# A hybrid attention layer: x given transposed beside x, weights laid out chunk by chunk, squares of x moved behind the first product

## The chip, the cores and the metric

The kernel runs on one core of a Trainium2 chip. The metric is device time in microseconds (us) of one execution; lower is better. The engines named below: TensorE (PE, with its weight loads as PEld), VectorE (DVE), ScalarE (ACT), GpSimd (POOL), and SyncE (SP), whose queue issues most transfers.

## What is computed

One decoder layer on x of 256 rows by 1024 columns, float32: an RMS norm, one wide projection, causal softmax attention with 8 heads of 64 (with 256 rows there is one key block, so the block choice selects nothing), gated linear attention with 4 heads, a merge by sigmoid gates, an output projection, the residual and a final RMS norm. Cut to what matters here:

```python
h = rms_norm(x, norm_in_g[layer])              # x * rsqrt(mean(x*x) + eps) * g
proj = jnp.einsum('bsd,de->bse', h, w_in[layer])
(mq, mk, mv, mgate, gq, gk, gv, ggate, gfg, ga, gb) = jnp.split(proj, split_pts, axis=-1)
...
oa = oa.transpose(0, 2, 1, 3).reshape(B, S, MOBA_WIDTH) * jax.nn.silu(mgate)
...
merged = (jax.nn.sigmoid(ga + b_merge[layer, 0]) * ya
          + jax.nn.sigmoid(gb + b_merge[layer, 1]) * yb)
x = x + jnp.einsum('bsd,de->bse', merged, w_out[layer])
return rms_norm(x, norm_f_g)
```

## The kernel before

**Products in three parts.** Each float32 product is made of three matmuls in the type float32r: both operands are split into a rounded part and a rest, `hi` and `lo` for weights, `xh` and `xl` for x, and hi·xh, hi·xl and lo·xh are added up in PSUM (`three`, L709). A weight chunk is loaded into a ring of five buffers (`raw`, L152), then cast on ACT to `hi` (L174) and subtracted on DVE to `lo` (L175), into rings of five each. `load_to(n)` and `split_to(n)` issue loads and splits up to chunk n - 1; `prefetch(i)` calls both some chunks ahead. All loads of chunks go through SP's queue.

**Chunks and groups.** `group` (L115) cuts the weights. Group mg (kind K) has 8 chunks, 0 to 7, of 128 rows by 512 columns, one for each k (a slice of 128 of the 1024 columns of x); they lie in a buffer of their own, `first`. Group gg (kind G) has chunks 8 to 11, two k each, 528 columns; gqk has chunks 12 to 15; then come mq, mk, mv, gv, ga, gb, the two projections and the output. TensorE runs the groups in this order.

**The start.** x is loaded in five pieces between the chunks of mg (L193), five matmuls on zeros follow (`warm`, L235), the norm's weights come as 8 rows and are turned into columns of `vecs` by a transpose (L270). `x_part(k)` (L246) transposes the slice k of x by two TensorE transposes into PSUM, multiplies it with the norm's weight into `xh` on ACT, and makes `xl` on DVE. In the mg loop (L716) every k runs 12 matmuls, and after two of its four column blocks `x_part(k + 2)` and `split_to` are issued. `squares` (L260, ACT) is issued at k = 5 and k = 6.

**The norm's factor.** It is not multiplied into x, but into the results. `gates_mg` (L332) is started after the mg loop: `rms` makes rs = (mean + eps)^-0.5, the power on POOL (L268); two `diag` tiles; a transpose of `b_merge`; four short matmuls `ones` x `diag` that spread rs over all partitions (L343); a copy to `rB` on ACT (L345); four multiplications `mgz` of mg's results with rB (L348); sigmoid and so on.

**The order.** The order on every engine is that of the program, which plans it with a clock of its own: a matmul of n columns adds n/2400, a side function's `yield t` lets it go on 0.9 t later, and side functions advance only at a `tick`. In gg there is a tick after each k (12 matmuls of 264 columns, L747). After gg the program waits with ticks alone, and no product of a group, until `gates_mg` has issued its last step (`wait_for("mg")`, L748); then the results of gg are read and gqk follows.

**PSUM.** `small` has four banks: they go in turn to the zero matmuls, to mg's blocks 0, 1 and 2, then again to a part of gg, and then to gqk's first half, which so gets the bank of mg's block 0.

Of the kernel before, what the change touches and what calls it, by code (L numbers as in the profile page):

```python
# [10 lines left out]
F32 = mybir.dt.float32  # L11
# [3 lines left out]
AF = mybir.ActivationFunctionType  # L15
# [4 lines left out]
P = 128  # L20
S = 256
NT = S // P
D = 1024
KD = D // P
# [50 lines left out]
    }  # L75


@with_exitstack
def layer(ctx, tc, x, norm_in_g, w_in, b_merge, w_fg2, b_fg, gla_g, w_pa, w_pb, w_out, norm_f_g,
          rope, causal, sums, masks, out):  # L80
    nc = tc.nc
    one = ctx.enter_context(tc.tile_pool(name="one", bufs=1))
    ring = ctx.enter_context(tc.tile_pool(name="ring", bufs=4))
# [11 lines left out]
    def transpose(out, in_, identity):  # L95
        nc.tensor.transpose(out, in_, identity)
        clock[0] += 0.11

    def f32(ap):
        return ap.bitcast(F32)  # L100
# [4 lines left out]
    def bank(name, tag="acc", bufs=3):  # L105
        return psum.tile([P, 512], F32, name=name, tag=tag, bufs=bufs)
# [1 line left out]
    def small(name):  # L108
        return bank(name, "small", 4)


    chunks = []
    groups = []

    def group(kind, name, src, c0, n, nk, step=2):  # L115
        ids = []
        if kind == "F":
            parts = [(c0 + p, 256, k0, 4) for p in range(0, n, 256) for k0 in range(0, nk, 4)]
        else:
            parts = [(c0, n, k0, step) for k0 in range(0, nk, step)]  # L120
        for c, w, k0, k in parts:
            ids.append(len(chunks))
            chunks.append(dict(src=src, c0=c, n=w, k0=k0, nk=k))
        groups.append(dict(kind=kind, name=name, ids=ids, nk=nk))

    group("K", "mg", w_in, C_MG, 512, KD, 1)
    group("G", "gg", w_in, C_GG, 528, KD)
    group("F", "gqk", w_in, C_GQ, 512, KD)
    group("F", "mq", w_in, C_MQ, 512, KD)
    group("F", "mk", w_in, C_MK, 512, KD)  # L130
    group("T", "mv", w_in, C_MV, 512, KD)
    group("T", "gv", w_in, C_GV, 512, KD)
    group("F", "ga0", w_in, C_GA, 512, KD)
    group("F", "ga1", w_in, C_GA + 512, 512, KD)
    group("F", "gb0", w_in, C_GB, 512, KD)
    group("F", "gb1", w_in, C_GB + 512, 512, KD)
    for h in range(2):
        group("F", f"pa{h}", w_pa, h * 512, 512, 4)
        group("F", f"pb{h}", w_pb, h * 512, 512, 4)
    oids = {}  # L140
    for half in range(2):
        for n in range(2):
            for k in range(4 * half, 4 * half + 4, 2):
                oids[n, k // 2] = len(chunks)
                chunks.append(dict(src=w_out, c0=n * 512, n=512, k0=k, nk=2))

    WMAX = 1056
    RAW, SPLIT = 5, 5
# [3 lines left out]
    def load_to(n):  # L152
        while loaded[0] < min(len(chunks), n):
            c = chunks[loaded[0]]
            size = c["nk"] * c["n"]
            if loaded[0] < KD:
                c["raw"] = first[:, loaded[0], :]
            else:
                raw = ring.tile([P, WMAX], F32, name="raw", bufs=RAW)
                c["raw"] = raw[:, :size]  # L160
            nc.sync.dma_start(
                c["raw"].rearrange("p (k n) -> p k n", n=c["n"]),
                c["src"][c["k0"] * P:(c["k0"] + c["nk"]) * P, c["c0"]:c["c0"] + c["n"]].rearrange(
                    "(k p) n -> p k n", p=P),
            )
            loaded[0] += 1

    def split_to(n):
        while done[0] < min(len(chunks), n):
            c = chunks[done[0]]  # L170
            size = c["nk"] * c["n"]
            hi = ring.tile([P, WMAX], F32R, name="hi", bufs=SPLIT)
            lo = ring.tile([P, WMAX], F32R, name="lo", bufs=SPLIT)
            nc.scalar.copy(hi[:, :size], c["raw"])  # L174
            nc.vector.tensor_sub(lo[:, :size], c["raw"], f32(hi[:, :size]))  # L175
            c["hi"] = hi[:, :size].rearrange("p (k n) -> p k n", n=c["n"])
            c["lo"] = lo[:, :size].rearrange("p (k n) -> p k n", n=c["n"])
            done[0] += 1
# [5 lines left out]

    xt = one.tile([P, NT, D], F32, name="xt")
    xr = x.rearrange("(t p) d -> p t d", p=P)
    grow = one.tile([8, P], F32, name="grow")
    brow = one.tile([16, P], F32, name="brow")  # L190
    nc.scalar.dma_start(grow, norm_in_g.rearrange("(k p) -> k p", p=P))
    first = one.tile([P, KD, 512], F32, name="first", tag="EX")
    for k0, k1 in ((0, 1), (1, 2), (2, 4), (4, 6), (6, 8)):  # L193
        nc.sync.dma_start(xt[:, :, k0 * P:k1 * P], xr[:, :, k0 * P:k1 * P])
        load_to(k1)

    ropet = one.tile([P, 2, S], F32, name="ropet")
# [3 lines left out]
    fgw = one.tile([32, 256], F32, name="fgw")  # L201
    ggb = one.tile([P, GDV], F32, name="ggb")
    small_loads = [
        (brow, b_merge.rearrange("n (k p) -> (n k) p", p=P)),
        (flat(ropet), rope),
        (ggb, gla_g.to_broadcast([P, GDV])),
        (fgw[0:RANK, :], w_fg2),
# [3 lines left out]
        (causalt, causal),  # L211
    ]
    load_to(KD + 2)
    for dst, src in small_loads[:6]:
        nc.sync.dma_start(dst, src)
    load_to(KD + RAW)

# [13 lines left out]
    def warm(n):  # L231
        for _ in range(n):
            nc.tensor.matmul(idle, zero[:, :P], zero, start=True, stop=True)

    warm(5)  # L235


    xh = one.tile([P, KD, S], F32R, name="xh", tag="xh")
    xl = one.tile([P, KD, S], F32R, name="xl", tag="xl")
    vecs = one.tile([P, 24], F32, name="vecs")  # L240
    def vectors(rows, r0, n):
        vp = bank("vp")
        transpose(vp[:, :n], rows, ident[:n, :n])
        nc.vector.tensor_copy(vecs[:, r0:r0 + n], vp[:, :n])

    def x_part(k):  # L246
        xp = bank(f"xp{k}")[:, :S]
        for t in range(NT):
            transpose(xp[:, t * P:(t + 1) * P], xt[:, t, k * P:(k + 1) * P], ident)
        nc.scalar.activation(xh[:, k, :], xp, AF.Copy, scale=vecs[:, k:k + 1])  # L250
        nc.vector.scalar_tensor_tensor(xl[:, k, :], xp, vecs[:, k:k + 1], f32(xh[:, k, :]),
                                       op0=OP.mult, op1=OP.subtract)

    ss = one.tile([P, NT, 2], F32, name="ss")
    rs = one.tile([P, NT], F32, name="rs")
    rB = one.tile([P, S], F32, name="rB")
    rB2 = rB[:, None, :].to_broadcast([P, 2, S])
    junk = one.tile([P, D], F32, name="junk", tag="m0")

    def squares(half):  # L260
        cs = slice(half * 512, half * 512 + 512)
        for t in range(NT):
            nc.scalar.activation(junk[:, :512], xt[:, t, cs], AF.Square, accum_out=ss[:, t, half:half + 1])

    def rms():
        nc.vector.tensor_add(rs, ss[:, :, 0], ss[:, :, 1])
        nc.vector.tensor_scalar(rs, rs, 1.0 / D, EPS, op0=OP.mult, op1=OP.add)
        nc.gpsimd.tensor_tensor(rs, rs, mhalf[:, :NT], op=OP.pow)  # L268

    vectors(grow, 0, 8)  # L270
    for k in range(2):
        split_to(k + 1)
        x_part(k)
    warm(2)


    vals = {}
# [52 lines left out]
    halves64 = [slice(0, 64), slice(64, 128)]  # L330

    def gates_mg(ps):  # L332
        rms()
        yield 3.5
        diag = [work.tile([P, P], F32, name=f"diag{t}", bufs=1) for t in range(NT)]
        for t in range(NT):
            nc.vector.tensor_scalar(diag[t], ident, rs[:, t:t + 1], None, op0=OP.mult)
        yield 1.5
        transpose(ps[2][:, S:S + 16], brow, ident[:16, :16])
        nc.vector.tensor_copy(vecs[:, 8:24], ps[2][:, S:S + 16])  # L340
        r = ps[3][:, S:]
        for t in range(NT):
            mm(r[:, t * P:(t + 1) * P], ones, diag[t], start=True, stop=True)  # L343
        yield 0.7
        nc.scalar.copy(rB, r)  # L345
        yield 0.7
        for f in range(4):
            nc.vector.tensor_mul(mgz[:, f, :], ps[f][:, :S], rB)  # L348
        nc.vector.tensor_mul(ropet, ropet, rB2)
        nc.vector.tensor_copy(sumsr, sumsf)  # L350
        yield 1.5
        sgm = one.tile([P, HP, S], F32, name="mgs", tag="m0")
        nc.scalar.activation(sgm, mgz, AF.Sigmoid)
        nc.gpsimd.tensor_mul(mgz, mgz, sgm)
        ready.add("mg")
# [358 lines left out]
    for g in groups:  # L714
        ids, name = g["ids"], g["name"]
        if g["kind"] == "K":  # L716
            ps = [small(f"{name}{f}") for f in range(3)] + [bank(f"{name}3", "side", 1)]
            for i in ids:
                c = chunks[i]
                k = c["k0"]  # L720
                if k == 5:
                    squares(0)
                if k == 6:
                    squares(1)
                for f in range(4):
                    fs = slice(f * P, (f + 1) * P)
                    if f == 2:
                        if k + 2 < KD:
                            x_part(k + 2)
                        split_to(i + SPLIT - 1 if k > 3 else i + 3)  # L730
                    three(ps[f][:, :S], c["hi"][:, 0, fs], c["lo"][:, 0, fs], xh[:, k, :], xl[:, k, :],
                          k == 0, k == KD - 1)
            start_side(gates_mg(ps))
        elif g["kind"] == "G":
            ps = {(t, b): (small if t and b else bank)(f"{name}{t}{b}") for t in range(NT) for b in range(2)}
# [27 lines left out]
        elif g["kind"] == "F":  # L763
            src = {"pa": (oah, oal), "pb": (obh, obl)}.get(name[:2], (xh, xl))
            if name == "mq":
                for dst, given in small_loads[6:]:
                    nc.sync.dma_start(dst, given)
            if name == "ga0":
                sg["ga"] = one.tile([P, KD, S], F32, name="sa", tag="m0")
# [75 lines left out]
    for t in range(NT):  # L845
# [13 lines left out]
        nc.scalar.dma_start(out[t * P:(t + 1) * P, :512], yn[:, t, :512])  # L859


_INS = ["x", "norm_in_g", "w_in", "b_merge", "w_gla_fg2", "b_gla_fg", "gla_norm_g", "w_proj_a", "w_proj_b",
        "w_out", "norm_f_g"]
_ROWS = ("b_gla_fg", "gla_norm_g", "norm_f_g")


# [25 lines left out]
```

## Time and profile before

| | us |
|---|---|
| median of 3 runs | 212.03 |
| lowest and highest | 211.34, 213.53 |
| the profiled execution | 211.96 |
| its span in the trace | 210.2 |
| TensorE busy in the span | 201.3 |
| VectorE, ScalarE, GpSimd busy | 143.1, 122.2, 31.2 |

The span runs from the first to the last instruction; the execution's time is 1.8 us longer. A timeline row gives start and duration. Matmuls are pipelined, so the distance between their starts is what one costs, and the duration shown is longer. TensorE is busy for 96% of the span; DMA engines moved 35.39 MB.

### The profile page before, as it was taken

To read this page: it belongs to the slowest core of one execution; us is meant where nothing else is said; L and a number is where in the kernel's file an instruction comes from. 1 tells how busy PE (TensorE), PEld (TensorE's weight loads), DVE (VectorE), ACT (ScalarE), POOL (GpSimd) and SP (SyncE) were. 2 spreads that over 40 slices of the span, in tenths; PEclk is the share of its full clock that TensorE was granted. 3 is DMA by queue.
4 is the path that set the end of the run, shared out by engine and by line. 5 is a ranking of instruction groups with operands and counts; after the bars stand their busy time and mean duration, and the time that the engine had idled before them with its cause. 6 is when DMAs were issued, how large, how long until landed. Compare 5 with 4: busy or idle time off the path is not lost.

```text
span 210.2 us, 4226 instructions
## 1 busy us (share of the span) xinstructions
PE 201.3 (96%) x1683; PEld 184.4 (88%) x1683; DVE 143.1 (68%) x261; ACT 122.2 (58%) x205; POOL 31.2 (15%) x31
## 2 busy tenths in 40 slices
PE   5999999999999999999999999999999999999980
PEld 1899999899999988877889889999999999989870
DVE  1666778969536899977569954757552969745371
ACT  3559926871999984236968433947554544541241
POOL 2000034800214540130001000100000040420011
PEclk9999999999999999999999999999999999999997
DMA  5999697494364556663342363754655485600022
GB/s 137 340 390 333 196 315 221 117 310 147 100 194 116 146 160 189 197 207 100 104 124 79 100 201 108 237 195 137 180 165 185 147 256 199 198 4 2 0 100 100
DMA packets 28502, 35.39 MB, mean 168 GB/s; under 512 B 1306, under 2 KB 21443, under 8 KB 28483
## 3 DMA queue, kind: packets, MB, share of 16 engines
q1 hardware_dynamic: 28178, 34.60, 53.4%
q10 hardware_dynamic: 304, 0.53, 0.7%
q8 instruction: 13, 0.21, 0.4%
q14 instruction: 7, 0.05, 0.1%
HBM read 34.08 MB, written 1.05 MB: 167 GB/s over the span
## 4 chain that ended last, share of the span: by engine, by line
PE 88%; DVE 4%; issue 3%; DMA 2%; SPq 0%; ACT 0%; POOLq 0%; POOL 0%
PE gb L91 11%; PE po L91 8%; PE ga L91 8%; PE mg L91 6%; PE gg L91 6%; PE gv L91 6%; PE gqk L91 5%; PE mk L91 5%; PE mq L91 5%; PE mv L91 5%; PE pa L91 5%; PE pb L91 5%; PE pv L91 2%; DMA xt<-in_x_dram 2%; PE a L91 2%
## 5 line engine op out<-in xcount | busy, mean ns | idle before, releaser
L175 DVE TENSOR_TENSOR lo<-raw,hi 128x1024 fp32r<-128x1024 f32 (+1 forms) x56 | 71.8, 1291 | 21.0 <-ACT hi L174 21.0
L174 ACT CAST hi<-raw 128x1024 fp32r<-128x1024 f32 (+1 forms) x56 | 57.7, 1048 | 20.7 <-PE po L91 6.3
L91 PE MATMUL ga<-xh,hi 128*128 128x256 f32 x64 | 18.5, 288 | 0.0
L91 PE MATMUL gb<-xh,hi 128*128 128x256 f32 x64 | 18.0, 282 | 0.0
L91 PE MATMUL gb<-xl,hi 128*128 128x256 f32 x64 | 18.0, 281 | 0.0
L91 PE MATMUL gb<-xh,lo 128*128 128x256 f32 x64 | 18.0, 281 | 0.0
L91 PE MATMUL ga<-xl,hi 128*128 128x256 f32 x64 | 18.0, 281 | 0.0
L91 PE MATMUL ga<-xh,lo 128*128 128x256 f32 x64 | 18.0, 280 | 0.0
L91 PE MATMUL po<-lo,mh 128*128 128x512 f32 (+1 forms) x40 | 14.0, 350 | 0.0
L91 PE MATMUL po<-hi,mh 128*128 128x512 f32 (+1 forms) x40 | 14.0, 350 | 0.0
L91 PE MATMUL po<-hi,ml 128*128 128x512 f32 (+1 forms) x40 | 14.0, 350 | 0.0
L614 POOL TENSOR_TENSOR m<-m,sa 128x512 f32<-128x512 f32 x4 | 6.0, 1500 | 46.4 <-ACT hi L174 35.5
L91 PEld LDWEIGHTS ga<-xh,hi 128*128 128x128 f32 x64 | 12.1, 188 | 0.9 <-issue 0.8
L555 ACT ACTIVATE sm<-sm,mx 128x128 f32<-128x128 f32 (+1 forms) x16 | 7.1, 444 | 9.7 <-DVE mx L551 9.7
L91 PEld LDWEIGHTS ga<-xl,hi 128*128 128x128 f32 x64 | 12.1, 189 | 0.0
L91 PEld LDWEIGHTS gb<-xh,hi 128*128 128x128 f32 x64 | 12.1, 189 | 0.0
L91 PEld LDWEIGHTS ga<-xh,lo 128*128 128x128 f32 x64 | 12.1, 188 | 0.0
L91 PEld LDWEIGHTS gb<-xh,lo 128*128 128x128 f32 x64 | 12.1, 188 | 0.0
L91 PEld LDWEIGHTS gb<-xl,hi 128*128 128x128 f32 x64 | 12.1, 188 | 0.0
L91 PE MATMUL mg<-xh,hi 128*128 128x256 f32 x32 | 10.6, 331 | 0.0
L91 PE MATMUL mg<-xl,hi 128*128 128x256 f32 x32 | 9.7, 305 | 0.0
L91 PE MATMUL mg<-xh,lo 128*128 128x256 f32 x32 | 9.6, 299 | 0.0
(197 smaller groups left out, 600.4 us busy)
## 6 DMA issues: line engine op xcount, KB each, us to landing
raw<-in_w_in_dram SPq DMA_DIRECT2D x36, 512.0 KB, 3.7
raw<-in_w_out_dram SPq DMA_DIRECT2D x8, 512.0 KB, 4.9
raw<-in_w_in_dram SPq DMA_DIRECT2D x4, 528.0 KB, 5.8
first<-in_w_in_dram SPq DMA_DIRECT2D x8, 256.0 KB, 5.8
raw<-in_w_proj_a_dram SPq DMA_DIRECT2D x4, 512.0 KB, 3.4
raw<-in_w_proj_b_dram SPq DMA_DIRECT2D x4, 512.0 KB, 4.2
xt<-in_x_dram SPq DMA_DIRECT2D x3, 256.0 KB, 5.7
late<-in_norm_f_g_dram SPq DMA_DIRECT2D x1, 512.0 KB, 5.1
```

What stands on the lines that cost most here:

```text
L91: nc.tensor.matmul(out, lhsT, rhs, start=start, stop=stop)
L174: nc.scalar.copy(hi[:, :size], c["raw"])
L175: nc.vector.tensor_sub(lo[:, :size], c["raw"], f32(hi[:, :size]))
L555: nc.scalar.activation(sm[:, cs], sm[:, cs], AF.Exp, bias=mx[:, t:t + 1], scale=0.125, accum_out=den[:, t:t + 1])
L614: nc.gpsimd.tensor_add(m, m, cut(sg["ga"]))
```

## The change

x comes in twice: transposed (`xT`, 1024 by 256) and plain. The transposed x is loaded into `xs` in five pieces where the plain x was; the plain x, which the squares and the residual need, is loaded in two pieces of 512 KB behind chunk 9 and ahead of the small tables and of chunks 10 to 12. `x_part` reads `xs` and has no transposes. The norm's weights and `b_merge` come as one array of 24 columns on ACT's queue, and their two transposes go, with one small load on SP's queue. All weight chunks lie in DRAM one behind the other, each partition's part in one piece. Eight zero matmuls run at the start instead of five, and two later ones go. In the mg loop `x_part` and `split_to` are issued ahead of each k's matmuls; k = 0 runs all hi·xh first, then hi·xl, then lo·xh. The squares are issued by `gates_mg`, ahead of `rms`, with a yield of 1.5 behind each pair. The array is laid out on the host, outside the time. Other lines of the diff (names of arrays, `plan` taken out of `layer`) change nothing on the chip.

```diff
+    for c in chunks:
+        c["at"] = at
+        at += P * c["nk"] * c["n"]
...
             nc.sync.dma_start(
-                c["raw"].rearrange("p (k n) -> p k n", n=c["n"]),
-                c["src"][c["k0"] * P:(c["k0"] + c["nk"]) * P, c["c0"]:c["c0"] + c["n"]].rearrange(
-                    "(k p) n -> p k n", p=P),
-            )
+                c["raw"], weights[c["at"]:c["at"] + P * size].rearrange("(p n) -> p n", p=P))
...
+    vecs = one.tile([P, 24], F32, name="vecs")
+    nc.scalar.dma_start(vecs, columns)
+    xs = one.tile([P, KD, S], F32, name="xs", tag="m0")
+    xTr = xT.rearrange("(k p) s -> p k s", p=P)
...
-    nc.scalar.dma_start(grow, norm_in_g.rearrange("(k p) -> k p", p=P))
...
-        nc.sync.dma_start(xt[:, :, k0 * P:k1 * P], xr[:, :, k0 * P:k1 * P])
+        nc.sync.dma_start(xs[:, k0:k1, :], xTr[:, k0:k1, :])
         load_to(k1)
...
-        (brow, b_merge.rearrange("n (k p) -> (n k) p", p=P)),
...
     load_to(KD + 2)
-    for dst, src in small_loads[:6]:
+    for t in range(NT):
+        nc.sync.dma_start(xt[:, t], xr[:, t])
+    for dst, src in small_loads[:5]:
         nc.sync.dma_start(dst, src)
     load_to(KD + RAW)
...
-    warm(5)
+    warm(8)
...
     def x_part(k):
-        xp = bank(f"xp{k}")[:, :S]
-        for t in range(NT):
-            transpose(xp[:, t * P:(t + 1) * P], xt[:, t, k * P:(k + 1) * P], ident)
-        nc.scalar.activation(xh[:, k, :], xp, AF.Copy, scale=vecs[:, k:k + 1])
-        nc.vector.scalar_tensor_tensor(xl[:, k, :], xp, vecs[:, k:k + 1], f32(xh[:, k, :]),
+        nc.scalar.activation(xh[:, k, :], xs[:, k, :], AF.Copy, scale=vecs[:, k:k + 1])
+        nc.vector.scalar_tensor_tensor(xl[:, k, :], xs[:, k, :], vecs[:, k:k + 1], f32(xh[:, k, :]),
                                        op0=OP.mult, op1=OP.subtract)
...
         for t in range(NT):
-            nc.scalar.activation(junk[:, :512], xt[:, t, cs], AF.Square, accum_out=ss[:, t, half:half + 1])
+            junk = work.tile([P, 512], F32, name="junk", tag="t512", bufs=4)
+            nc.scalar.activation(junk, xt[:, t, cs], AF.Square, accum_out=ss[:, t, half:half + 1])
...
-    vectors(grow, 0, 8)
     for k in range(2):
+        x_part(k)
         split_to(k + 1)
-        x_part(k)
-    warm(2)
...
     def gates_mg(ps):
+        for half in range(2):
+            squares(half)
+            yield 1.5
         rms()
         yield 3.5
...
-        transpose(ps[2][:, S:S + 16], brow, ident[:16, :16])
-        nc.vector.tensor_copy(vecs[:, 8:24], ps[2][:, S:S + 16])
...
-                if k == 5:
-                    squares(0)
-                if k == 6:
-                    squares(1)
-                for f in range(4):
-                    fs = slice(f * P, (f + 1) * P)
-                    if f == 2:
-                        if k + 2 < KD:
-                            x_part(k + 2)
-                        split_to(i + SPLIT - 1 if k > 3 else i + 3)
-                    three(ps[f][:, :S], c["hi"][:, 0, fs], c["lo"][:, 0, fs], xh[:, k, :], xl[:, k, :],
-                          k == 0, k == KD - 1)
+                if k + 2 < KD:
+                    x_part(k + 2)
+                split_to(i + SPLIT - 1 if k > 3 else i + 3)
+                parts = [(c["hi"], xh), (c["hi"], xl), (c["lo"], xh)]
+                todo = [(f, j) for f in range(4) for j in range(3)]
+                for f, j in sorted(todo, key=lambda n: n[::-1]) if k == 0 else todo:
+                    w, v = parts[j]
+                    mm(ps[f][:, :S], w[:, 0, f * P:(f + 1) * P], v[:, k, :], k == 0 and j == 0, k == KD - 1 and j == 2)
```

## Rows read from the trace of the kernel before

**Rows 1.** The page's busy times: us, share of the span, instructions.

```profile
PE 201.3 (96%) x1683; PEld 184.4 (88%) x1683; DVE 143.1 (68%) x261; ACT 122.2 (58%) x205; POOL 31.2 (15%) x31
```

**Rows 2.** The chain that ended last, 0 to 45 us: start, us, what.

```profile
6.88 1.33 PE mg L91 x6
8.21 0.43 PE xp L96 x2
...
10.75 0.22 PE xp L96 x2
...
12.61 1.41 PE mg L91 x12
...
17.50 3.80 PE mg L91 x30
...
21.46 8.94 PE gg L91 x71
...
30.55 0.64 PE mg L91 x4
31.19 2.92 PE gg L91 x24
```

**Rows 3.** Timeline, 0 to 26 us: start, us, engine, line, operation, out<-in, [idle before].

```profile
4.98 0.62 ACT L174 CAST hi<-first 128x512 fp32r<-128x512 f32 x1 [2.10 <-DMA first<-in_w_in_dram]
...
6.32 0.78 PE L91 MATMUL mg<-xh,hi 128*128 128x256 f32 x1
...
9.71 0.41 PE L91 MATMUL mg<-xh,hi 128*128 128x256 f32 x1
...
10.11 0.28 PE L91 MATMUL mg<-xh,lo 128*128 128x256 f32 x1
```

**Rows 4.** Timeline of ACT, 16 to 48 us.

```profile
17.31 0.63 ACT L263 ACTIVATE junk<-xt 128x512 f32<-128x512 f32 x1
...
18.69 0.46 ACT L250 ACTIVATE xh<-xp,vecs 128x256 fp32r<-128x256 f32 x1
...
21.39 5.10 ACT L174 CAST hi<-raw 128x1056 fp32r<-128x1056 f32 x5
...
31.23 0.37 ACT L345 COPY rB<-mg 128x256 f32<-128x256 f32 x1 [2.64 <-PE mg L91]
...
37.53 0.35 ACT L365 COPY gfT<-gft 16x256 f32<-16x256 f32 x1
```

**Rows 5.** Timeline of DVE, 16 to 48 us.

```profile
26.00 0.15 DVE L266 TENSOR_TENSOR rs<-ss 128x2 f32<-128x2 f32 x1
...
26.30 1.23 DVE L175 TENSOR_TENSOR lo<-raw,hi 128x1024 fp32r<-128x1024 f32 x1
28.13 0.48 DVE L337 TENSOR_SCALAR diag<-ident,rs 128x128 f32<-128x128 f32 x2 [0.61 <-POOL rs L268]
...
31.81 1.41 DVE L348 TENSOR_TENSOR mgz<-mg,rB 128x256 f32<-128x256 f32 x4
```

**Rows 6.** Timeline of POOL, 16 to 48 us.

```profile
26.44 1.66 POOL L268 TENSOR_TENSOR rs<-rs,mhalf 128x2 f32<-128x2 f32 x1 [24.43 <-DVE rs L267]
```

**Rows 7.** Windows: stretch, busy by engine, granted clock, DMA share, GB/s last.

```profile
2.00:8.00 6.00, 4.99 (x17) 2.91 (x16) 1.88 (x5) 2.85 (x6) 0.01 (x1) 1.00 0.95 249
...
0.00:16.00 16.00, 13.80 (x79) 11.19 (x80) 7.47 (x16) 7.49 (x15) 1.41 (x8) 1.00 0.89 290
8.00:16.00 8.00, 8.00 (x62) 8.00 (x62) 5.17 (x10) 4.02 (x9) 0.00 (x0) 1.00 1.06 390
16.00:21.00 5.00, 5.00 (x42) 4.83 (x42) 3.12 (x5) 4.94 (x12) 0.00 (x0) 1.00 0.98 334
```

**Rows 8.** Timeline of SP, 0 to 46 us: one of the small issues.

```profile
10.16 0.35 SPq L215 DMA_DIRECT2D brow<-in_b_merge_dram  x1
```

**Rows 9.** Timeline of TensorE, 28 to 62 us: the first gqk and fg matmuls.

```profile
33.95 0.28 PE L91 MATMUL gqk<-xh,hi 128*128 128x256 f32 x1
...
39.88 1.13 PE L91 MATMUL fg<-fgw,gfT 17*128 17x256 f32 x4
```

More of the change, by code (lines that the diff above doesn't have):

```diff
@@ L75, in constants, with plan, group, laid_out @@
     }
+def plan():
+    chunks = []
+    groups = []
+    def group(kind, name, src, c0, n, nk, step=2):
+        ids = []
+        if kind == "F":
+            parts = [(c0 + p, 256, k0, 4) for p in range(0, n, 256) for k0 in range(0, nk, 4)]
+        else:
+            parts = [(c0, n, k0, step) for k0 in range(0, nk, step)]
+        for c, w, k0, k in parts:
+            ids.append(len(chunks))
+            chunks.append(dict(src=src, c0=c, n=w, k0=k0, nk=k))
+        groups.append(dict(kind=kind, name=name, ids=ids, nk=nk))
+    group("K", "mg", "w_in", C_MG, 512, KD, 1)
+    group("G", "gg", "w_in", C_GG, 528, KD)
+    group("F", "gqk", "w_in", C_GQ, 512, KD)
+    group("F", "mq", "w_in", C_MQ, 512, KD)
+    group("F", "mk", "w_in", C_MK, 512, KD)
+    group("T", "mv", "w_in", C_MV, 512, KD)
+    group("T", "gv", "w_in", C_GV, 512, KD)
+    group("F", "ga0", "w_in", C_GA, 512, KD)
+    group("F", "ga1", "w_in", C_GA + 512, 512, KD)
+    group("F", "gb0", "w_in", C_GB, 512, KD)
+    group("F", "gb1", "w_in", C_GB + 512, 512, KD)
+    for h in range(2):
+        group("F", f"pa{h}", "w_proj_a", h * 512, 512, 4)
+        group("F", f"pb{h}", "w_proj_b", h * 512, 512, 4)
+    oids = {}
+    for half in range(2):
+        for n in range(2):
+            for k in range(4 * half, 4 * half + 4, 2):
+                oids[n, k // 2] = len(chunks)
+                chunks.append(dict(src="w_out", c0=n * 512, n=512, k0=k, nk=2))
+    at = 0
+    for c in chunks:
+        c["at"] = at
+        at += P * c["nk"] * c["n"]
+    return chunks, groups, oids
+def laid_out(weights):
+    def chunk(src, c0, n, k0, nk, at):
+        w = weights[src][k0 * P:(k0 + nk) * P, c0:c0 + n]
+        return w.reshape(nk, P, n).transpose(1, 0, 2).reshape(-1)
+    return np.concatenate([chunk(**c) for c in plan()[0]])
 @with_exitstack
-def layer(ctx, tc, x, norm_in_g, w_in, b_merge, w_fg2, b_fg, gla_g, w_pa, w_pb, w_out, norm_f_g,
-          rope, causal, sums, masks, out):
+def layer(ctx, tc, x, xT, columns, weights, w_fg2, b_fg, gla_g, norm_f_g, rope, causal, sums, masks, out):
     nc = tc.nc
@@ L109, in small @@
         return bank(name, "small", 4)
[L112 to L145, printed above, removed]
+    chunks, groups, oids = plan()
     WMAX = 1056
@@ L183, in prefetch @@
         split_to(i + SPLIT - 1)
+    vecs = one.tile([P, 24], F32, name="vecs")
+    nc.scalar.dma_start(vecs, columns)
+    xs = one.tile([P, KD, S], F32, name="xs", tag="m0")
+    xTr = xT.rearrange("(k p) s -> p k s", p=P)
     xt = one.tile([P, NT, D], F32, name="xt")
     xr = x.rearrange("(t p) d -> p t d", p=P)
-    grow = one.tile([8, P], F32, name="grow")
-    brow = one.tile([16, P], F32, name="brow")
-    nc.scalar.dma_start(grow, norm_in_g.rearrange("(k p) -> k p", p=P))
     first = one.tile([P, KD, 512], F32, name="first", tag="EX")
     for k0, k1 in ((0, 1), (1, 2), (2, 4), (4, 6), (6, 8)):
-        nc.sync.dma_start(xt[:, :, k0 * P:k1 * P], xr[:, :, k0 * P:k1 * P])
+        nc.sync.dma_start(xs[:, k0:k1, :], xTr[:, k0:k1, :])
         load_to(k1)
@@ L233, in warm @@
             nc.tensor.matmul(idle, zero[:, :P], zero, start=True, stop=True)
-    warm(5)
+    warm(8)
     xh = one.tile([P, KD, S], F32R, name="xh", tag="xh")
     xl = one.tile([P, KD, S], F32R, name="xl", tag="xl")
[L240 to L244, printed above, removed]
-    def x_part(k):
-        xp = bank(f"xp{k}")[:, :S]
-        for t in range(NT):
-            transpose(xp[:, t * P:(t + 1) * P], xt[:, t, k * P:(k + 1) * P], ident)
-        nc.scalar.activation(xh[:, k, :], xp, AF.Copy, scale=vecs[:, k:k + 1])
-        nc.vector.scalar_tensor_tensor(xl[:, k, :], xp, vecs[:, k:k + 1], f32(xh[:, k, :]),
+    def x_part(k):
+        nc.scalar.activation(xh[:, k, :], xs[:, k, :], AF.Copy, scale=vecs[:, k:k + 1])
+        nc.vector.scalar_tensor_tensor(xl[:, k, :], xs[:, k, :], vecs[:, k:k + 1], f32(xh[:, k, :]),
                                        op0=OP.mult, op1=OP.subtract)
@@ L257, in layer @@
     rB2 = rB[:, None, :].to_broadcast([P, 2, S])
-    junk = one.tile([P, D], F32, name="junk", tag="m0")
     def squares(half):
@@ L332, in gates_mg @@
     def gates_mg(ps):
+        for half in range(2):
+            squares(half)
+            yield 1.5
         rms()
@@ L765, in layer @@
             if name == "mq":
-                for dst, given in small_loads[6:]:
+                for dst, given in small_loads[5:]:
                     nc.sync.dma_start(dst, given)
@@ L859, in layer @@
         nc.scalar.dma_start(out[t * P:(t + 1) * P, :512], yn[:, t, :512])
-_INS = ["x", "norm_in_g", "w_in", "b_merge", "w_gla_fg2", "b_gla_fg", "gla_norm_g", "w_proj_a", "w_proj_b",
-        "w_out", "norm_f_g"]
-_ROWS = ("b_gla_fg", "gla_norm_g", "norm_f_g")
 def kernel(**inputs):
@@ L874, in given @@
     def given(name, a):
+        a = np.ascontiguousarray(a)
         arrays[f"in_{name}_dram"] = a
         args.append(nc.dram_tensor(f"in_{name}_dram", a.shape, mybir.dt.from_np(a.dtype), kind="ExternalInput").ap())
-    for name in _INS:
-        a = np.ascontiguousarray(inputs[name])
-        if name == "norm_f_g":
-            a = a[None]
-        elif name not in _ROWS:
-            a = a[0]
-        given(name, np.ascontiguousarray(a))
+    put = {name: np.asarray(a) for name, a in inputs.items()}
+    x = put["x"][0]
+    given("x", x)
+    given("xT", x.T)
+    given("columns", np.concatenate([put["norm_in_g"].reshape(KD, P), put["b_merge"].reshape(2 * KD, P)]).T)
+    given("weights", laid_out({name: put[name][0] for name in ("w_in", "w_proj_a", "w_proj_b", "w_out")}))
+    given("w_gla_fg2", put["w_gla_fg2"][0])
+    given("b_gla_fg", put["b_gla_fg"])
+    given("gla_norm_g", put["gla_norm_g"])
+    given("norm_f_g", put["norm_f_g"][None])
     for name, a in constants().items():
-        given(name, np.ascontiguousarray(a))
+        given(name, a)
     args.append(nc.dram_tensor("out_0_dram", (S, D), F32, kind="ExternalOutput").ap())
```

## The prediction

> **What bounds the kernel now.** I read the page's busy times first, then the chain of work that ended last, then the timelines of the first 48 us engine by engine, then the windows for the transfers. TensorE is busy for 201.3 of 210.2 us [rows 1]. So two things can shorten this kernel: work taken off TensorE, and holes in its stream or a slow pace of it. The chain shows what the change can reach there [rows 2]. Twelve mg matmuls take 1.41 us, 0.1175 each, and between one k and the next stand two transposes of x: 0.43 us the first time, 0.22 us six times, 1.75 us together. At the start the pace is another: six matmuls take 1.33 us, 0.22 each. For 256 columns 0.21 us is 1.2 GHz, and 0.1175 us is near 2.4 GHz; the timeline puts the change of pace between 9.71 and 10.11, though the window table's granted clock reads 1.00 throughout [rows 3, 7]. The first real matmul starts at 6.32, 3.6 us ahead of that change; the cast of the first weight chunk, which it needs, started at 4.98, when its load landed [rows 3].
>
> **Part 1, transposes and first matmul (a gain in the mg stage).** Gone are 16 transposes of x: the 1.75 us above. The first matmul now needs xh of k=0, whose input is a plain load ahead of the weight chunk, and hi of chunk 0, cast 0.62 us from 4.98 [rows 3]. The multiplication of x no longer queues behind that cast on ACT, so I start at 5.4 instead of 6.3: 0.9 us earlier. The load of `columns` (12 KB in 96-byte rows, on ACT's queue) has no row like it; at nothing it hides behind the 4.98, and landing 1 us after that load it would take back the 0.9. I take nothing: the queue holds nothing else. The pace change I leave at 9.9 us, though eight idle matmuls instead of five could bring it forward. From 5.4 then: 21 matmuls at 0.213 until 9.9, 75 at 0.1175 = 8.8, end near 18.7. Before, the mg stage ended near 21.2, where the gg rows begin [rows 2]: 2.5 us gained there.
>
> **Part 2, bytes.** x is read twice, so 1.05 MB more go through SP's queue, placed ahead of the small tables and of weight chunks 10, 11, 12. Two more issues at about 0.35 us each against one removed [rows 8] are covered by the backlog in the queue. Before, 290 GB/s over 16 us is 4.64 MB [rows 7]. In the new order the bytes up to the end of chunk 11 are 1.05 (xT) + 2.10 (mg chunks) + 1.08 (chunks 8, 9) + 1.05 (x) + 0.60 (tables) + 1.08 (chunks 10, 11) = 6.96 MB, so 2.32 MB remain at 16 us. At the 390 GB/s of 8 to 16 us they land at 22.0, at the 334 of 16 to 21 us at 23.0 [rows 7]. From 2 to 8 us the engines were 0.95 busy at only 249 GB/s [rows 7]; the first two pieces of x, now in 1 KB rows instead of 512 B, and the contiguous chunks may lift that. At 390 GB/s from 2 us on, 6 x (390 - 249)/390 = 2.2 us would be saved, at worst nothing. I take a quarter of that, 0.6, and half of the microsecond between 22.0 and 23.0: chunk 11 lands at 21.9. The bounds are 19.8 and 23.0, the likelier part 20.8 to 23.0. The Trainium skill (HBM Reference, Specifications) speaks against extra bytes more strongly: 358 GB/s effective per core. The 390 above is more, so the measurement decides; by 358 instead of 390 from 16 us on, an estimate, chunk 11 would land 0.5 us later and the sum below end at 211.8.
>
> The contiguous layout of the later chunks I price at nothing: TensorE waits for no load after the mg stage, since casts run several chunks ahead of it. If that cover were gone, TensorE would wait at a chunk for the load's lateness, in full.
>
> **Part 3, the squares (a loss, and the decisive one).** The four squares move from the mg loop to the side work that runs during gg. They sit in ACT's order: cast of chunk 10 (issued with k=7 of mg), cast of 11, two squares, cast of 12, two squares, cast of 13. The timeline of ACT keeps the order of the program, idling where the next one isn't ready: it sits 2.64 us before rB at 31.23, until matmuls release it [rows 4]. So x itself may be there near 17.6 us (5.28 of the bytes above, at 390 GB/s), but its squares stand behind casts whose chunks x's own load has pushed back.
>
> When the rest is issued follows from the planner's clock. One k of gg adds 12 x 264/2400 = 1.32; a yield of 1.5 costs 0.9 x 1.5 = 1.35 and so misses the next tick by 0.03 and takes two. Squares come at ticks 1 and 3, rms at tick 5 (3.15 later is tick 8), diag at tick 8, the last of gg, and everything after it while no product is left: the four matmuls with `diag`, the copy rB, the multiplications mgz. (The same count for before gives the matmuls at tick 6 of 8, with 24 gg matmuls behind; the chain shows 24 behind them [rows 2].) The PSUM bank that the first gqk matmul needs is mg's first, free after the first mgz. What was covered by 24 gg matmuls of 2.92 us now stands bare.
>
> The sum, from chunk 11's landing: cast of 11 1.02 (five in 5.10), two squares 1.38 (17.31 to 18.69), cast of 12 1.02, two squares 1.38, cast of 13 1.02 [rows 4]; lo of 13 1.23; rs to the start of the power 0.44; the power 1.66 on POOL; diag 0.48 [rows 5, 6]; matmuls 0.64 [rows 2]; rB 0.37 [rows 4]; first mgz 1.41/4 = 0.35 [rows 5]; 0.45 for nine handovers like the 0.04 between the matmuls' end at 31.19 and rB at 31.23. That is 11.4 us: 21.9 + 11.4 = 33.3 for the first gqk matmul. TensorE alone would be there earlier: 18.7 + 96 x 0.122 (71 gg in 8.94 us is 0.126, 24 in 2.92 is 0.122 [rows 2]) = 30.4. It then waits, with 0.64 us of matmuls inside, some 2.3 us. In the trace of before the first gqk matmul starts at 33.95 [rows 9]. So the 2.5 us gained in mg, with the short transpose of b_merge that goes, are nearly given back at one point.
>
> **After that point** the order is the planner's old one. ACT's burst (sigmoids, casts of 15 and 16, copy gfT) starts some 1.9 us later against gqk: rB ran 2.7 us ahead of it (31.23 against 33.95), now 0.8. gfT ended at 37.88, 2.0 us ahead of the matmuls at 39.88 that read it [rows 4, 9]; that margin just covers the shift, and if it did not, TensorE would wait for the difference, at most some 0.5 us.
>
> **Sum.** 33.3 - 33.95 = -0.65; I add nothing downstream. The profiled execution took 211.96 us for a span of 210.2, close to the median of 212.03; so 211.3, and with chunk 11 between 20.8 and 23.0 it is 210.2 to 212.4.
>
> **Rivals.**
> A, the squares are hidden. If the loads run nearly at 390 GB/s from 2 us on, so that chunk 11 lands at 20.4 or earlier, diag is ready when gg ends at 30.4, and gqk starts at 30.4 + 0.64 + 0.41 + 0.45 = 31.9: 2.0 us gained, 209.9. If the eight idle matmuls also bring the fast pace forward to the first matmul, 21 matmuls each save 0.096, another 2.0 us at most, which the loads cut to about 1: down to 208.9. For it: the 249 GB/s, so there is room. Against: three quarters of that room would have to be won, and the engines were as busy then as later [rows 7]. Chance 0.25.
> B, the wait cools TensorE (the other side, slower). The hole before gqk is 1.4 us, then 0.64 us of matmuls, then 0.9 us. If the pace falls to the level of the start, the next matmuls take 0.213 instead of 0.1175 until it rises again; the start shows 3.6 us of slow matmuls [rows 3], 17 x 0.096 = 1.6 us: 212.9. It decides once the pace falls at all. For it: the first matmuls of the kernel are slow, so TensorE does not have the fast pace by itself. Against: no hole in a fast stretch of this trace shows what it does to the pace. Chance 0.12.
> C, the loads come later (chunk 11 past 23.0, for instance because the queue does not hold 390 GB/s with 4 KB rows of x between) or ACT's burst makes fg and the casts late: 0.5 to 1.5 us more, 212.6 to 213.4. Chance 0.13.
> D, the gain of mg stays and the end moves by it because the wait ends with something other than mgz (a bank that is free anyway): 211.96 - 2.6 = 209.4 (the 2.5 and the short transpose). I see no other free bank in the order of allocation. Chance 0.04.
>
> **How the numbers follow.** The forecast, 211.3, has 0.46 and its own range from 210.2 to 212.4. A range from 209.4 to 213.3 takes in the forecast, C, about half of A and most of B, some 8 in 10. Faster by over 1% is below 209.85: somewhat over half of A and all of D, 0.20. Slower by over 1% is above 214.15: B together with C, or a slow pace that lasts, 0.07. The rest, 0.73, is within 1%, about what a measurement of this kernel can tell from no change.
>
> **What would show it.** Right: mg's matmuls stand back to back and end near 18.7; ACT idles before the cast of chunk 10, some microseconds, ended by its load; the squares start near 23; the four matmuls with diag stand behind the last gg matmul, after a hole of 1 to 2 us ended by diag on DVE, and gqk follows a second hole ended by mgz; gqk starts between 33 and 34.5. Wrong: squares before 21 us, or diag ready before gg ends (A); matmuls of gqk at 0.21 us (B); holes in gg before the casts of chunks 10 and 11 (C); gqk right behind the diag matmuls (D). If the mg stage does not end some 2 us earlier, part 1 is wrong.

## The result and the profile after

The changed kernel is slower: 213.89 us (median of 20 executions, 212.03 to 215.57) against 211.76 us for the kernel before (20 executions), a ratio of 1.0091 with a 95% interval of 1.0067 to 1.0116. (Ratio and interval leave out the two longest executions of the changed kernel, 215.57 and 215.31.) The profiled execution took 215.57 us, span 213.8, and is the longest of the twenty; its span is 3.6 us above that of before, and nearly all of it is there by the time of the first fg matmuls (43.4 us against 39.9).

The chain of work that ended last, 0 to 60 us, in the kernel after (start, us, what); it answers to [rows 2]:

```profile
9.80 7.28 DMA xt<-in_x_dram
...
17.10 6.80 DMA raw<-in_weights_dram
...
24.00 1.07 ACT hi L188
...
29.46 1.23 DVE lo L189
...
31.05 1.64 POOL rs L275
...
32.71 0.30 DVE diag L345
...
33.05 0.96 PE mg L142 x4
...
34.04 0.38 ACT rB L351
...
34.44 0.44 DVE mgz L354
...
34.92 5.46 PE gqk L142 x24
...
40.60 2.85 PE gqk L142 x24
43.45 1.06 PE fg L142 x4
```

Before, this stretch of the chain was TensorE alone. Now it runs over two loads, three casts with the squares between them, DVE, POOL and back, and TensorE enters at 33.05. The waits of TensorE show the holes (engine, line, what it waited for: us in total, times, longest):

```profile
PE mg L142 <- DVE diag L345: 1.9, 1, 1.9
...
PE gqk L142 <- DVE mgz L354: 0.9, 1, 0.9
PE gg L142 <- DVE lo L189: 0.9, 1, 0.9
```

ACT's timeline of the kernel after answers to [rows 4]: the cast of chunk 10 waits 5.70 us for its load, chunk 11 follows, and only then come the squares, though the first half of x had landed at 17.1 and the second at 19.8. (The timeline puts the last 0.26 us before the cast of chunk 11 down to TensorE; the chain above has its load, which landed at 23.9.)

```profile
22.67 1.07 ACT L188 CAST hi<-raw 128x1056 fp32r<-128x1056 f32 x1 [5.70 <-DMA raw<-in_weights_dram]
24.00 1.07 ACT L188 CAST hi<-raw 128x1056 fp32r<-128x1056 f32 x1 [0.26 <-PE gg L142]
24.98 0.63 ACT L270 ACTIVATE junk<-xt 128x512 f32<-128x512 f32 x1
...
27.78 0.62 ACT L270 ACTIVATE junk<-xt 128x512 f32<-128x512 f32 x1
```

The windows show what the holes did. The columns are those of [rows 7]; the last three are the granted clock, the DMA share and GB/s:

```profile
31.00:32.00 1.00, 0.11 (x1) 0.00 (x0) 1.00 (x1) 0.00 (x0) 0.95 (x1) 1.00 0.89 311
32.00:33.00 1.00, 0.00 (x0) 0.00 (x0) 0.39 (x3) 0.00 (x0) 0.68 (x1) 1.00 0.73 188
33.00:34.00 1.00, 0.95 (x4) 0.65 (x4) 0.19 (x1) 0.00 (x0) 0.00 (x0) 0.69 0.89 303
...
39.00:40.00 1.00, 1.00 (x7) 1.00 (x6) 0.64 (x2) 1.00 (x2) 1.00 (x2) 0.50 0.00 0
40.00:41.00 1.00, 1.00 (x9) 0.92 (x9) 1.00 (x1) 0.65 (x2) 1.00 (x2) 0.90 0.00 0
```

After two microseconds with next to no matmul the granted clock falls to 0.50, which is 1.2 GHz, from about 33 to 40 us. The first 24 gqk matmuls take 5.46 us, the next 24 take 2.85 (chain above). That is rival B.

The gain in mg is there too, larger than forecast. TensorE's timeline of the kernel after:

```profile
4.68 1.22 PE L142 MATMUL mg<-xh,hi 128*128 128x256 f32 x4
...
6.35 0.64 PE L142 MATMUL mg<-xh,lo 128*128 128x256 f32 x4
...
17.91 0.29 PE L142 MATMUL gg<-hi,xh 128*128 128x264 f32 x1
```

gg starts at 17.91 instead of about 21.2 [rows 2]: 3.3 us won in mg. It is spent in the waits above, 0.9 us inside gg, 1.9 ahead of the diag matmuls and 0.9 behind them, and in the diag matmuls themselves, which no longer run between gg matmuls and already at the falling clock (0.96 us). gqk starts at 34.92 instead of 33.95 [rows 9], 0.97 later; its slow first half costs another 5.46 - 2.85 = 2.6. Together 3.6 us, the whole difference of the spans.

Most executions lose less to the clock than this one. Its mean granted clock is 0.977. Of the twenty, five have 0.976 or 0.977 and a median of 214.94 us, twelve 0.982 to 0.985 and 213.8 us, three 0.997 and 212.63 us. The traces kept show the clock at 0.50 in two places only, behind these holes and in the last microseconds of the execution, so the lower mean clocks stand for this fall: it costs most executions some 1.1 us, and not 2.6.

### The profile page after: what moved, and what is told of

It reads as the page before. It is cut to its first block, busy times and chain, and to the rows that moved or that the text cites. A ratio compares the mean times of both kernels' runs of the same rounds, so it can differ in the third digit from the quotient of the medians.

```text
span 213.8 us, 4191 instructions
## 1 busy us (share of the span) xinstructions
PE 201.8 (94%) x1666; PEld 184.5 (86%) x1666; DVE 143.5 (67%) x259; ACT 123.0 (58%) x205; POOL 35.8 (17%) x31
## 4 chain that ended last, share of the span: by engine, by line
PE 75%; DMA 9%; DVE 5%; issue 3%; ACT 3%; SPq 1%; POOL 1%; POOLq 0%; ACTq 0%
PE gb L142 11%; PE ga L142 8%; PE po L142 8%; PE gqk L142 7%; PE gv L142 5%; PE mk L142 5%; PE mq L142 5%; PE mv L142 5%; PE pa L142 5%; PE pb L142 5%; DMA xt<-in_x_dram 3%; DMA raw<-in_weights_dram 3%; DMA xs<-in_xT_dram 3%; PE pv L142 2%; PE a L142 2%
## 5 line engine op out<-in xcount | busy, mean ns | idle before, releaser
L189 DVE TENSOR_TENSOR lo<-raw,hi 128x1024 fp32r<-128x1024 f32 (+1 forms) x56 | 72.7, 1303 | 27.6 <-ACT hi L188 27.4
L700 POOL TENSOR_TENSOR kT<-kT,z 128x512 f32<-128x512 f32 x2 | 10.5, 5226 | 7.2 <-DVE z L699 4.3
L142 PE MATMUL gqk<-xh,hi 128*128 128x256 f32 x32 | 10.4, 326 | 0.9 <-DVE mgz L354 0.9
L142 PE MATMUL gqk<-xl,hi 128*128 128x256 f32 x32 | 10.1, 314 | 0.0
```

Source lines behind the costliest of these rows:

```text
L142: nc.tensor.matmul(out, lhsT, rhs, start=start, stop=stop)
L700: nc.gpsimd.tensor_add(dst, dst, z)
```

## The experiments

Theory 1: gqk's start is set by the squares, which stand on ACT behind casts of chunks that x's second load has pushed back; the hole this leaves makes TensorE's clock fall, and that costs a second time. Rivals: the bytes of the second x cost by themselves wherever the squares stand; the clock falls for another reason; the new layout changes the loads.

**The clock.** Zero matmuls fill the two holes, and nothing else is touched (e1_fill; `fill(to, n)` is n matmuls of 256 columns on zeros):

```diff
         r = ps[3][:, S:]
+        fill(ps[2][:, S:], 14)
         for t in range(NT):
             mm(r[:, t * P:(t + 1) * P], ones, diag[t], start=True, stop=True)
+        fill(ps[2][:, S:], 7)
```

> The changed kernel with zero matmuls (256 columns, results unused) put into TensorE's two holes ahead of gqk: 14 before the matmuls with diag, 7 behind them. The chain of ACT, DVE and POOL is not touched. Theory 1 (the chain sets when gqk starts, and the hole ahead of it costs a second time by the slow pace that follows): gqk starts at 34.9 as in the changed kernel, the granted clock stays 1.00 from 30 to 45 us, fg starts near 41.0 instead of 43.45, and the time is 2.5 us below the changed kernel's runs with the slow stretch: 211.4. Theory 2 (the pace falls for another reason, such as time or the load of the transfers): the clock still falls to 0.5 near 33 us and the time stays near 213.9.

Measured: 212.40 us (10 executions), 1.0034 of before (1.0005 to 1.0063); no execution of the ten has a mean granted clock under 0.990, while 17 of the 20 of the changed kernel lie between 0.976 and 0.985. TensorE's timeline of e1_fill:

```profile
30.74 1.70 PE L255 MATMUL mg<-zero 128*128 128x256 bf16 x14
32.87 0.71 PE L142 MATMUL mg<-diag,ones 128*128 128x128 f32 x4 [0.43 <-DVE diag L349]
```

Its chain, and then its windows (columns as above):

```profile
34.50 3.12 PE gqk L142 x24
```

```profile
36.00:40.00 4.00, 4.00 (x36) 3.97 (x35) 3.36 (x9) 4.00 (x8) 3.39 (x2) 1.00 0.00 1
```

gqk starts about where it did (34.50), the clock stays at 1.00 from 30 to 45 us, the first 24 gqk matmuls take 3.12 us instead of 5.46, and fg starts at 40.6 instead of 43.4. So the fall comes from the holes. My 211.4 was too low, because I took the 2.5 us, read from the longest execution, off the median. Against before, the ratio went from 1.0091 to 1.0034: without the fall the changed kernel is some 1.2 us faster. What is left against before is gqk's later start.

**The order.** Squares, rms and diag are issued ahead of the cast of chunk 10; the loads stay (e2_order; `factor` is squares(0), squares(1), rms and the two diag):

```diff
+                if k == KD - 1:
+                    factor()
                 split_to(i + SPLIT - 1 if k > 3 else i + 3)
...
     def gates_mg(ps):
-        for half in range(2):
-            squares(half)
-            yield 1.5
-        rms()
-        yield 3.5
...
-        yield 1.5
+        yield 5.5
```

> The changed kernel with the squares, rms and diag issued at k=7 of mg, ahead of the cast of chunk 10; the loads are as in the changed kernel, x twice. Theory 1 (the squares' place behind the casts of chunks 10 and 11 is what delays gqk): squares run at 17.1 to 19.9 us, as soon as x has landed; the matmuls with diag stand inside gg with no wait; the 0.9 us hole before the third k-pair of gg, for lo of chunk 10, remains; gqk starts at 31.2, no slow pace, 209.2 us, faster than the kernel before by 1.2%. Theory 3 (the bytes of the second x are the loss, wherever the squares stand): gqk not before 33.5 and 211.5 us or more.

Measured: 208.90 us (4 executions), 0.9886 of before (0.9854 to 0.9918), faster than both kernels. ACT's timeline of e2_order:

```profile
17.48 0.63 ACT L270 ACTIVATE junk<-xt 128x512 f32<-128x512 f32 x1 [0.57 <-DMA xt<-in_x_dram]
...
21.45 1.08 ACT L188 CAST hi<-raw 128x1056 fp32r<-128x1056 f32 x1 [2.02 <-DMA raw<-in_weights_dram]
```

Its chain:

```profile
25.49 0.44 PE mg L142 x4
25.93 4.40 PE gg L142 x36
30.34 2.85 PE gqk L142 x24
```

The squares run in time that ACT had spent waiting, the diag matmuls stand inside gg, and gqk starts at 30.34, 4.6 us before the changed kernel. Of the holes, 0.5 us is left, for lo of chunk 10. The same bytes are loaded in the same order, so theory 3 falls. Not all of the 4.6 us is the order: in this execution the loads ran faster, 320 GB/s over the first 16 us against 298, and chunk 10 was cast 1.2 us earlier. With the same order at 297 GB/s (e7_warm5, below) gqk starts 3.8 us before the changed kernel.

**The loads as well.** On top of e2_order, the second x goes behind chunk 10, the tables behind chunk 12, the squares behind the cast of chunk 10 (e3_both):

```diff
-    load_to(KD + 2)
+    load_to(KD + 3)
     for t in range(NT):
         nc.sync.dma_start(xt[:, t], xr[:, t])
+    load_to(KD + RAW)
     for dst, src in small_loads[:5]:
         nc.sync.dma_start(dst, src)
-    load_to(KD + RAW)
```

> As e2_order, and the second x is loaded behind chunk 10 instead of ahead of it, the small tables behind chunk 12; the squares stand behind the cast of chunk 10. Theory 1: chunk 10 lands near 19 us, the hole of 0.9 us in gg goes, the squares run from about 20 us on, gqk starts at 30.3, and the time is 208.3 us. Theory 3: no better than e2_order.

Measured: 208.83 us (4 executions), 0.9873 of before (0.9847 to 0.9900): no different from e2_order. ACT's timeline of e3_both:

```profile
16.98 1.08 ACT L188 CAST hi<-raw 128x1056 fp32r<-128x1056 f32 x1 [0.25 <-DMA raw<-in_weights_dram]
19.75 0.63 ACT L270 ACTIVATE junk<-xt 128x512 f32<-128x512 f32 x1 [1.68 <-DMA xt<-in_x_dram]
...
26.51 1.05 ACT L188 CAST hi<-raw 128x1024 fp32r<-128x1024 f32 x1 [1.62 <-DMA raw<-in_weights_dram]
27.47 0.36 ACT L352 COPY rB<-mg 128x256 f32<-128x256 f32 x1
```

Its chain:

```profile
30.56 3.10 PE gqk L142 x24
```

The hole in gg went, as expected, but x landed later, the cast of chunk 13 waited 1.62 us for its load, rB and the cast of chunk 14 stood behind it on ACT, mgz behind lo of chunk 14 on DVE, and gqk waited 0.3 us for mgz. A hole was moved, not removed.

**The second x.** It is loaded behind chunk 12, the squares keep their place and read the transposed x, so that nothing waits for it (e4_x_late; it leaves out the right factor of the norm, so only its time is of use):

```diff
     load_to(KD + 2)
-    for t in range(NT):
-        nc.sync.dma_start(xt[:, t], xr[:, t])
     for dst, src in small_loads[:5]:
         nc.sync.dma_start(dst, src)
     load_to(KD + RAW)
+    for t in range(NT):
+        nc.sync.dma_start(xt[:, t], xr[:, t])
...
-            nc.scalar.activation(junk, xt[:, t, cs], AF.Square, accum_out=ss[:, t, half:half + 1])
+            nc.scalar.activation(junk, flat(xs[:, 4 * half + 2 * t:4 * half + 2 * t + 2, :]), AF.Square, accum_out=ss[:, t, half:half + 1])
```

> The changed kernel with the second x loaded behind chunk 12, and the squares, left in their place, taken from the transposed x, so that they wait for no load; the norm's factor is therefore another number than the reference's. It measures what the second x costs by its place in the queue. Theory 1: chunks 10 and 11 land about 2.5 us earlier, near 20.1 and 21.3, the cast of chunk 11 starts when the buffer and the load allow, about 21.4; the chain of 11.3 us from there ends at 32.7 for gqk; a hole of some 1.5 and one of 0.9 us remain, so the pace may or may not fall: 210.8 without, 213.2 with the slow stretch. Theory 3: no hole, gqk near 31, 209.3 us.

Measured: 210.69 us (10 executions), 0.9983 of before (0.9955 to 1.0012). ACT's timeline of e4_x_late, then TensorE's waits, then the chain:

```profile
18.64 1.07 ACT L188 CAST hi<-raw 128x1056 fp32r<-128x1056 f32 x1 [1.85 <-DMA raw<-in_weights_dram]
20.89 1.08 ACT L188 CAST hi<-raw 128x1056 fp32r<-128x1056 f32 x1 [1.18 <-DMA raw<-in_weights_dram]
```

```profile
PE mg L142 <- DVE diag L345: 1.5, 1, 1.5
...
PE gqk L142 <- DVE mgz L354: 0.9, 1, 0.9
```

```profile
32.32 3.12 PE gqk L142 x24
```

The casts of chunks 10 and 11 start 4.0 and 3.1 us earlier than in the changed kernel, and gqk 2.6 us earlier. But two holes remain, 1.5 and 0.9 us, because the squares still stand behind the casts. So the second x's place in the queue is worth 2.6 us of gqk's start and the order 3.8 to 4.6; with the order of e2_order the same bytes cost little more than its hole of 0.5 us. The holes here bring the clock down only at times: six of the ten executions have a mean granted clock of 0.990 or more and take 210.3 to 210.8 us, the other four 0.978 to 0.985 and 211.7 to 214.0 us.

**The layout alone.** The kernel before with the weights laid out chunk by chunk (e5_layout_alone); its one line of effect is the load:

```diff
-                c["raw"].rearrange("p (k n) -> p k n", n=c["n"]),
-                c["src"][c["k0"] * P:(c["k0"] + c["nk"]) * P, c["c0"]:c["c0"] + c["n"]].rearrange(
-                    "(k p) n -> p k n", p=P),
+                c["raw"], weights[c["at"]:c["at"] + P * size].rearrange("(p n) -> p n", p=P))
```

> The kernel before with one part of the change: the weights laid out chunk by chunk, x plain only, with its transposes. Theory 1 prices the layout at nothing, since TensorE waits for no load behind the mg stage: 211.0 to 211.8 where before has 211.3 to 211.8, gqk still starting near 33.9. Theory 4 (the layout itself slows or quickens the loads in a way that reaches TensorE): over 1 us of difference either way, and waits of casts for loads behind 20 us.

Measured: 211.37 us (10 executions), 0.9977 of before (0.9947 to 1.0007). The page counts 12117 DMA packets instead of 28502, and the rate from 8 to 16 us is 391 GB/s where it was 390 [rows 7]. No difference in time that can be told from none, as priced. But gqk did not start near 33.9 in its trace:

```profile
32.82 0.28 PE L143 MATMUL gqk<-xh,hi 128*128 128x256 f32 x1
```

The cast of chunk 0 started at 4.39 instead of 4.98 and the pace changed near 8.3 instead of 10. Whether the layout does this, one trace does not tell; the medians differ by 0.3 us. The casts of chunks 13 and 14 waited 0.2 and 1.4 us for their loads, behind 20 us, which theory 4 had as a sign; TensorE waited for neither.

**The late chunks.** Chunk 13 and later are held on SP's queue until chunk 11 is cast (e6_hold):

```diff
+        if i == KD:
+            split_to(i + SPLIT - 1)
+            nc.scalar.copy(seen, held)
+            nc.sync.dma_start(held, x[0:P, 0:1])
         load_to(i + SPLIT + RAW - 2)
```

> The changed kernel with the loads of chunk 13 and later held on SP's queue until the cast of chunk 11 is done (a tiny load that waits for an ACT copy behind that cast). It asks why chunks 10 and 11 landed at 22.65 and 23.9, when the bytes ahead of chunk 11 (6.96 MB) had been moved some 2.3 us earlier. Theory L1 (loads issued behind them take engine time from them): they land near 20.6 and 22.0, and gqk starts some 1.9 us earlier, near 33.0. Theory L2 (a load is complete when the slowest of its engines is, whatever is queued behind): they land at 22.6 and 23.9 as in the changed kernel, with a falling rate in the last microseconds; gqk near 34.9 or later.

Measured: one execution, 214.27 us. ACT's timeline of e6_hold, then its windows:

```profile
22.31 1.07 ACT L188 CAST hi<-raw 128x1056 fp32r<-128x1056 f32 x1 [5.38 <-DMA raw<-in_weights_dram]
23.60 1.08 ACT L188 CAST hi<-raw 128x1056 fp32r<-128x1056 f32 x1 [0.21 <-DMA raw<-in_weights_dram]
```

```profile
21.00:22.00 1.00, 1.00 (x11) 1.00 (x10) 0.00 (x0) 0.00 (x0) 0.00 (x0) 1.00 1.01 397
22.00:23.00 1.00, 1.00 (x10) 1.00 (x10) 0.00 (x0) 0.69 (x1) 0.00 (x0) 1.00 0.56 222
23.00:24.00 1.00, 1.00 (x10) 1.00 (x9) 0.58 (x1) 0.79 (x2) 0.00 (x0) 1.00 0.10 41
```

With nothing behind chunk 12, the casts start only 0.4 us earlier, where L1 asked for some 2. So the loads of chunk 13 and later are not what delays chunk 11; chunk 12 was not held and could still take engine time from it. From 23 us on the DMA engines are nearly idle, and yet chunk 11 lands only at 23.5. That it waits for the slowest of the 16 engines, as L2 says, fits the 0.10 but was not shown, since the trace here does not tell the engines apart. gqk starts at 34.50, and behind holes of 2.2 and 0.9 us the clock falls here too. Its chain:

```profile
34.50 4.58 PE gqk L142 x24
```

The mean granted clock is 0.983, as in most executions of the changed kernel, and the first 24 gqk matmuls take 4.58 us, 1.7 more than the next 24.

**The zero matmuls.** e2_order with five instead of eight, `warm(8)` turned into `warm(5)` (e7_warm5):

> e2_order with five zero matmuls at the start instead of eight, so that TensorE pauses about 2 us ahead of the first mg matmul instead of about none. Theory 5 (the three added ones bring the fast pace forward): the pace changes near 9 to 10 us instead of near 6.5, mg ends near 18.8 instead of 17.3 to 17.9, the hole for chunk 10 in gg goes, gqk starts 0.5 to 0.9 us later, 209.4 to 209.8. Rival: the pace changes at the same moment whatever ran before, 208.9.

Measured: 209.38 us (4 executions), 0.9878 of before (0.9825 to 0.9930). TensorE's timeline of e7_warm5, then its chain:

```profile
4.71 1.23 PE L142 MATMUL mg<-xh,hi 128*128 128x256 f32 x4 [1.21 <-ACT hi L188]
...
10.43 0.39 PE L142 MATMUL mg<-xh,lo 128*128 128x256 f32 x1
```

```profile
4.71 14.28 PE mg L142 x96
18.99 7.35 PE gg L142 x60
...
31.16 2.86 PE gqk L142 x24
```

With a hole of 1.2 us ahead of mg, the pace changes at 10.4 us, where it changed between about 4.7 and 7.1 us in the profiles of the changed kernel and of e1 to e4, with eight. The first gg matmul starts at 18.83 by the timeline, in e2_order at 17.28. Half of these 1.6 us comes back, since gg no longer waits for chunk 10: gqk starts at 31.16 against 30.34.

## Why the prediction was wrong

**Two steps failed: the landing of chunk 11 in part 2, and the weight of B.** From the forecast, 211.3, to the median, 213.89, it is 2.6 us. Part 2 is 1.6 of them, in gqk's start (33.3 by the sum, 34.92 in the trace). The rest, some 1.0, is the fall of the pace: the forecast added "nothing downstream" of gqk's start, and gave the fall 0.12. It happened in 17 of 20 executions. My argument for the low chance was that no hole in a fast stretch of the trace of before shows what it does; that is a reason for not knowing, not against. The holes were forecast as 1.4 and 0.9 us with 0.64 us of matmuls between, and came as 1.9, 0.9 and 0.96, so the test was a harder one than B's terms said. B's price of 1.6 us was not the mistake: the fall cost 2.6 us in the profiled execution, where 24 matmuls and more were slow and not 17, 1.7 in e6_hold, and 1.1 to 1.2 by the medians.

**Part 1 was right and too small.** 3.3 us instead of 2.5: the first matmul started at 4.68 instead of 5.4, since the cast of chunk 0 started at 4.01 instead of 4.98, and the pace changed some 4 us sooner, which e7_warm5 puts down to the three added zero matmuls. This gain went nowhere, because TensorE was not what set gqk's start.

**Part 2 was mis-sized by 2 us.** Chunk 11 was to land at 21.9, at worst 23.0, and landed at 23.9. The count of bytes was good: 298 GB/s over 16 us is 4.77 MB (4.64 before), so 2.19 MB remained, and at the 392 GB/s of 16 to 24 us they had been moved at 21.6, if the queue moves them in order. What I left out is the time from the last byte's turn in the queue to the landing of the whole chunk, 2.3 us here and 1.9 to 2.5 by the same count in e1_fill, e2_order, e6_hold and e7_warm5; e3_both has it too, some 1.4 us for chunk 10 (4.77 MB up to its end by its order, 4.96 MB moved by 16.0 us, cast at 16.98). What this time is made of stays open. A load was taken as done when the bytes ahead of it were done.

**Part 3 was right.** The 0.9 us hole inside gg, for which the sum had no term, cost nothing more, since the chain over ACT was later still. Order on ACT, ticks 1 and 3 for the squares, the diag matmuls behind the last gg matmul, gqk behind the first mgz: all as forecast. The chain from the landing of chunk 11 to gqk was 11.4 us by the sum and 11.0 in the trace (23.9 to 34.92). gqk's start was 33.3 by the sum, 34.92 in fact; the 1.6 between them is part 2's 2.0 less the chain's 0.4. With chunk 11 at 23.9 the sum gives 213.3, and with gqk's measured start 212.9, both without the fall; the 212.9 is near the three executions whose mean granted clock was 0.997, at 212.03, 212.63 and 213.03.

**The Trainium skill's 358 GB/s** (HBM Reference, Specifications), which spoke against the extra bytes, was not the reason: the rate was 392 GB/s from 16 to 24 us. **A** did not happen, though the earlier pace that it allowed for did; **D** did not. **C** did, in its first half: the load was late, for another reason than the one given.

## What to carry to other kernels

When work is moved behind a stage, price it from where it will stand in its engine's order, with the landing of every load that the instructions ahead of it wait for; half of x was there at 17.1 us, the rest at 19.8, and the first of it was read at 25. On a kernel whose TensorE is full, a hole costs twice if the clock falls after it. Here that happened in 4 of 10 executions with holes of 1.5 and 0.9 us and in 17 of 20 with 1.9 and 0.9, so a forecast with such holes needs the slow stretch in the sum, at its chance, and not only in a rival. And in these runs a load landed 1.4 to 2.5 us later than its bytes' turn in a full queue: take the delay from issue to landing from the rows, not the byte count alone.

## What the hardware showed that I had not expected

How small the holes are behind which the clock falls. The holes are read from one profiled execution of each kernel, the counts from the mean clocks of all. Holes of 1.9 and 0.9 us with the four diag matmuls between them: a mean clock of 0.985 or less in 17 of 20 executions. 1.5 and 0.9 us: in 4 of 10. 0.4 and 0.2 us: in none of 10. Where the edge lies between these, and which of the two holes decides, stays open. And at the start three zero matmuls of 0.43 us each, closing a hole of 1.2 us, moved the change of pace from 10.4 us to between 4.7 and 7.1; in e5_layout_alone, with five and a hole of 0.5 us, it came at 8.3. Whether the added matmuls or the closed hole does it, no run separates.
